# Queries turned two heads at a time, their squares summed by halving additions on POOL

## The chip, the cores and the metric

One core of a Trainium2 chip runs the whole kernel. The metric is the device time of one execution in microseconds (us). The engines are PE (TensorE, the matrix unit), ACT (ScalarE), DVE (VectorE), POOL (GpSimd) and SP (SyncE, which here only starts DMAs). Each engine works through its own queue in order, and they wait for each other by semaphores.

## What is computed

One layer of a bidirectional encoder over two sequences of 512 tokens with width 1024: an attention branch (16 heads of 64, four key and value heads, a window of 128 tokens to both sides) and a state-space branch run from the same normed input, are gated and added, and a squared-ReLU MLP follows. What matters here is the attention's queries:

```python
h = rms_norm(x, ln1)
proj = h @ w_in
q, k, v, u, g_att, g_ssm = jnp.split(proj, IN_SPLITS, axis=-1)
q = rms_norm(q.reshape(bsz, seq_len, N_HEADS, HEAD_DIM), q_gain)   # over each head's 64 numbers
k = rms_norm(k.reshape(bsz, seq_len, N_KV_HEADS, HEAD_DIM), k_gain)
...
s = einsum(q, k) * scale + bias      # then masked, with a sink logit, softmax, times v
```

## The kernel before

Matrix products are made in float32 precision from two parts: a number is split into a high part (rounded to the matrix unit's float32 format) and a low part (the rest), and three products (high by high, high by low, low by high) are added in PSUM. Where both parts of one operand fit on the partitions together, one product does two: a head has 64 numbers, so a query's high part lies on partitions 0 to 63 and its low part on 64 to 127, and the keys are held twice, once on either half (`kh` the high part in both halves, `kl` the low). A score matmul with `kh` and one with `kl` then give the sum of all four products, whichever half of the query lies on which rows.

The attention works in eight steps (four groups of four heads, two sequences each), and a step in four units of 128 query rows. A unit (class `Unit`) makes for each of its four heads the scores (`scores`, L970), the bias and the row's maximum (`largest`, DVE, L974), the exponentials (`exp`, ACT, L980), and, one unit later, turns the probabilities (`turn`, PE, L986), splits them into parts (`high`, ACT, L990; `low`, DVE, L995), multiplies by the values (`value`, PE, L1002) and adds the two halves (`lower_part`, ACT, L1006; `add`, DVE, L1012).

Beside it runs one query tile for the next step (class `Tile`): 128 rows by four heads of 64. Its way goes through all engines:

- `project`: 24 matmuls of 256 columns, spread over the unit (PE, L919)
- `square`: squares of the projection, scaled (ACT, L925), at the end of the unit
- `power`: sum of each head's 64 squares (DVE, L929), plus epsilon (POOL, L931), to the power of -0.5 (POOL, L932); at the start of the next unit
- `norm`: projection times that factor (DVE, L936), in that unit, behind two maxima, an addition and a low part on DVE
- `turn`: four transposes, one for each head (PE, L941), behind the fourth head's scores
- `high` and `low`: the copy with the gain (ACT, L946) and the rest (DVE, L949)

The order of the instructions on PE, ACT, DVE and POOL is the order in which the loop writes them out. At a unit's start stand `power`, low parts for a later stage (`y_lows`, POOL, L1066, from step 6 on), then `scores(0)`, `largest(0)` and so on. The core of a unit's loop is:

```python
project(6)
if n3:
    prev.low(0)
cur.exp(0)
cur.exp(1)
if rows and not rows.qn:
    rows.norm()
...
if rows:
    rows.turn()
```

POOL also copies the sink logits into each unit's row block (L962), copies keys once a step (L888), subtracts high parts of weights (L874, L786) and issues some DMAs (L1170). DVE has, from the second step on, two more operations of 1024 columns on SBUF in each step: the gate's multiplication at the end of the third unit (`gated`, L1047) and the one by the reciprocal sums at the end of the fourth (`multiply`, L1051). Ahead of the eight steps stands a front in which the four tiles of the first step are made between the projections of the values (`rows_block`, `v_evac`). In the eighth step there are no tiles.

Of the kernel before, what the change touches and what calls it, by code (L numbers as in the profile page):

```python
# [12 lines left out]
F32 = mybir.dt.float32  # L13
F32R = mybir.dt.float32r
I32 = mybir.dt.int32
AF = mybir.ActivationFunctionType
ALU = mybir.AluOpType
AX = mybir.AxisListType

P = 128  # L20
# [10 lines left out]
G = 4  # L31
HD = 64
# [32 lines left out]
def hybrid_layer(ctx, tc, x, x_t, w_kv, rel, onehot, w_qkv, w_ug, vectors, lam, coefs, w_glu, w_out, ln2,  # L65
                 w_up, w_down, out):
    nc = tc.nc
    V, S, PE, GP, SP = nc.vector, nc.scalar, nc.tensor, nc.gpsimd, nc.sync
# [12 lines left out]
    def acc():  # L81
        return ps_acc.tile([P, 512], F32, tag="acc", name="acc")
# [23 lines left out]
    ident = const.tile([P, P], F32, name="ident")  # L106
# [5 lines left out]
    bglu_sb, gain_q, gain_k, nsink = [vec[:, a:b] for a, b in ((0, 8), (8, 9), (9, 10), (10, 26))]  # L112
# [422 lines left out]
    with tc.tile_pool(name="hst", bufs=1) as hp:  # L535
        h = hp.tile([P, NCHUNK, 2, GROUPS, NSEQ], F32, name="h")
# [148 lines left out]
        with tc.tile_pool(name="ssmo", bufs=2) as sp:  # L685
# [54 lines left out]
            for q in range(GROUPS // SH):  # L740
# [7 lines left out]
                for g in range(SH):  # L748
                    o = ps[:, g * P:(g + 1) * P]
# [88 lines left out]
    with tc.tile_pool(name="att", bufs=2, reuse_waits="tile") as ap, tc.tile_pool(name="attc", bufs=1, reuse_waits="tile") as ac:  # L838
# [18 lines left out]
        weights, keys, queries, biases = {}, {}, {}, {}  # L857
# [48 lines left out]
        class Tile:  # L906
# [19 lines left out]

            def power(self):
                ms = small.tile([P, G], F32, tag="ms", name="ms")
                V.reduce_sum(ms, self.sq, axis=AX.X)  # L929
                self.rq = small.tile([P, G], F32, tag="rq", name="rq")  # L930
                GP.tensor_scalar_add(ms, ms, EPS)  # L931
                GP.tensor_tensor(self.rq, ms, neg_half[:, 0:G], op=ALU.pow)  # L932
# [4 lines left out]

            def turn(self):
                self.pt = self.pt or acc()
                for h in range(G):  # L940
                    PE.transpose(self.pt[0:64, h * P:(h + 1) * P], self.qn[:, h], ident)  # L941

            def high(self):
                self.ptv = self.pt[0:64].rearrange("p (h t) -> p h t", h=G)
                self.dst = queries[self.key][:, :, self.t * P:(self.t + 1) * P]
                S.activation(self.dst[0:64], self.ptv, AF.Copy, scale=gain_q[0:64])  # L946

            def low(self):
                V.scalar_tensor_tensor(self.dst[64:128], self.ptv, gain_q[0:64], self.dst[0:64].bitcast(F32),  # L949
                                       op0=ALU.mult, op1=ALU.subtract)  # L950

        class Unit:

# [149 lines left out]
        with tc.manual_schedule(engines={ET.PE, ET.DVE, ET.Activation, ET.Pool}):  # L1103
# [11 lines left out]
            ms, rk = [small.tile([P, NB * N_KV], F32, tag="rsum", name=n, bufs=2) for n in ("k_ms", "k_rs")]  # L1115
# [45 lines left out]
        with tc.manual_schedule(engines={ET.PE, ET.Activation, ET.DVE, ET.Pool}):  # L1161
            for i, (j, sq) in enumerate(steps):
# [4 lines left out]
                for qb in range(NB):  # L1167
                    if 1 <= i < 3:
                        t = (i - 1) * NB + qb
# [213 lines left out]
    with tc.tile_pool(name="rn2", bufs=2, reuse_waits="tile") as rn2:  # L1383
# [51 lines left out]
        def put_turned(sq, t, last=lambda: None, between=()):  # L1435
# [9 lines left out]
            def put(dst, src):  # L1445
                high(dst, src)
                next(inner, lambda: None)()
                low(dst, src)
# [10 lines left out]
            if not between:  # L1459
                S.copy(tt[0], x11)  # L1460
                high(B22, x22)
                V.tensor_sub(tt[0], x12, tt[0])
                low(B22, x22)
                high(T1, tt[0])
                V.tensor_sub(tt[1], x22, tt[0])
                low(T1, tt[0])
                high(T2, tt[1])
                S.copy(tt[0], x22)
                low(T2, tt[1])
                V.tensor_sub(tt[0], tt[0], x12)  # L1470
                high(T3, tt[0])
                V.tensor_sub(tt[1], tt[1], x21)
                high(T4, tt[1])
                last()
                low(T3, tt[0])
                low(T4, tt[1])
                xb.clear()
                return
# [47 lines left out]
        def parts(src, owed=None):  # L1526
            i = next(turn) % KT
            hi, lo = [q[:, i, :].rearrange("p (k n) -> p k n", k=4) for q in ring]
            S.copy(hi, src)
            low = lambda: V.tensor_sub(lo, src, hi.bitcast(F32))  # L1530
            low() if owed is None else owed.append(low)
            return hi, lo
# [325 lines left out]
```

## Time and profile before

| | us |
|---|---|
| median of 3 runs | 1445.42 (1445.25 to 1445.69) |
| the profiled execution | 1445.04 |
| its span, first instruction to last | 1443.3 |
| busy PE, DVE, ACT, POOL | 1435.6, 1094.9, 762.3, 244.1 |
| granted clock of the matrix unit | 1.00 throughout |

The attention with its front lies between 408 and 661 us of the span; ahead of it are the projections and the state-space scan, behind it the gated sum and the MLP. A row of the timeline gives the start and the length in us, the engine, the line, the operation, what it writes and reads, the shape and the number of instructions that the row merges; in brackets stand the idle time before it and what ended it. A row of the groups gives the count, the busy us, the mean ns of one, the idle time before and what ended it. The shape on a PE row is that of the weights (128\*64) and of the moving operand.

### The profile page before, as it was taken

To read this page: it belongs to the slowest core of one execution; us is meant where nothing else is said; L and a number is where in the kernel's file an instruction comes from. 1 tells how busy PE (TensorE), PEld (TensorE's weight loads), DVE (VectorE), ACT (ScalarE), POOL (GpSimd) and SP (SyncE) were. 2 spreads that over 40 slices of the span, in tenths; PEclk is the share of its full clock that TensorE was granted. 3 is DMA by queue.
4 is the path that set the end of the run, shared out by engine and by line. 5 is a ranking of instruction groups with operands and counts; after the bars stand their busy time and mean duration, and the time that the engine had idled before them with its cause. 6 is when DMAs were issued, how large, how long until landed. Compare 5 with 4: busy or idle time off the path is not lost.

```text
span 1443.3 us, 22044 instructions
## 1 busy us (share of the span) xinstructions
PE 1435.6 (99%) x7997; PEld 1228.0 (85%) x7997; DVE 1094.9 (76%) x1978; ACT 762.3 (53%) x1359; POOL 244.1 (17%) x396
## 2 busy tenths in 40 slices
PE   9999999999999999999999999999999999999998
PEld 8888888889999999988888888888888888888887
DVE  7999959995458999988976588777776597575644
ACT  7678861224448887894444255455454443333332
POOL 3144443004244432263100000000000000000000
PEclk9999999999999999999999999999999999999999
DMA  7356549529651533345552344444442983464341
GB/s 297 97 170 189 168 147 327 206 91 314 227 180 59 162 107 100 119 140 189 194 190 91 129 136 173 161 160 155 151 143 96 363 319 102 146 201 145 121 131 59
DMA packets 102204, 240.23 MB, mean 166 GB/s; under 512 B 12330, under 2 KB 25130, under 8 KB 102096
## 3 DMA queue, kind: packets, MB, share of 16 engines
q1 hardware_dynamic: 62304, 139.94, 29.9%
q0 software_dynamic: 16320, 48.28, 10.2%
q10 hardware_dynamic: 23472, 50.61, 9.5%
q8 instruction: 63, 1.03, 0.3%
q14 instruction: 45, 0.37, 0.1%
HBM read 169.02 MB, written 81.82 MB: 174 GB/s over the span
## 4 chain that ended last, share of the span: by engine, by line
PE 84%; DVE 8%; issue 4%; DMA 2%; ACT 1%; POOL 1%; DVEq 0%; SPq 0%; ACTq 0%; POOLq 0%
PE bank L118 14%; PE bank L120 14%; PE bank L119 14%; PE acc L187 9%; PE acc L125 6%; PE acc L919 5%; PE po L1002 2%; PE sps L970 2%; PE sps L641 2%; PE tps L986 2%; PE sps L753 2%; PE acc L120 2%; PE acc L119 2%; PE acc L118 2%; DVE t L716 2%
## 5 line engine op out<-in xcount | busy, mean ns | idle before, releaser
L187 PE MATMUL acc<-act,c_hi 128*128 128x512 f32 x768 | 243.7, 395 | 0.0
L119 PE MATMUL bank<-b_lo,a_hi 128*128 128x512 f32 (+1 forms) x449 | 174.4, 389 | 0.0
L120 PE MATMUL bank<-b_hi,a_lo 128*128 128x512 f32 (+1 forms) x449 | 174.4, 389 | 0.0
L118 PE MATMUL bank<-b_hi,a_hi 128*128 128x512 f32 (+1 forms) x449 | 174.4, 389 | 0.0
L187 PEld LDWEIGHTS acc<-act,c_hi 128*128 128x128 f32 x768 | 142.3, 188 | 27.8 <-ACT act L316 0.9
L1714 ACT CAST a_hi<-d_a 128x1024 fp32r<-128x1024 f32 x56 | 59.1, 1055 | 177.4 <-PE bank L119 173.2
L187 PE MATMUL acc<-act,c_lo 128*128 128x512 f32 x384 | 151.3, 394 | 0.0
L1715 DVE TENSOR_TENSOR a_lo<-d_a,a_hi 128x1024 fp32r<-128x1024 f32 x56 | 68.5, 1223 | 98.5 <-ACT a_hi L1714 98.5
L118 PE MATMUL bank<-act,act 128*128 128x512 f32 x368 | 143.2, 389 | 0.0
L119 PE MATMUL bank<-act,act 128*128 128x512 f32 x368 | 143.2, 389 | 0.0
L120 PE MATMUL bank<-act,act 128*128 128x512 f32 x368 | 143.2, 389 | 0.0
L919 PE MATMUL acc<-w_hi,act 128*128 128x256 f32 x512 | 114.0, 291 | 0.1
L119 PEld LDWEIGHTS bank<-b_lo,a_hi 128*128 128x128 f32 x449 | 84.3, 188 | 17.5
L120 PEld LDWEIGHTS bank<-b_hi,a_lo 128*128 128x128 f32 x449 | 84.3, 188 | 17.5
L118 PEld LDWEIGHTS bank<-b_hi,a_hi 128*128 128x128 f32 x449 | 84.3, 188 | 17.3
L919 PEld LDWEIGHTS acc<-w_hi,act 128*128 128x128 f32 x512 | 87.0, 189 | 4.0 <-PE sps L970 0.3
L187 PEld LDWEIGHTS acc<-act,c_lo 128*128 128x128 f32 x384 | 72.2, 188 | 14.7 <-DVE c_lo L178 0.8
L125 PE MATMUL acc<-act,gc_hi 128*128 128x512 f32 x256 | 81.2, 394 | 0.3 <-POOL act L1066 0.3
L118 PEld LDWEIGHTS bank<-act,act 128*128 128x128 f32 x368 | 69.1, 188 | 14.4
L120 PEld LDWEIGHTS bank<-act,act 128*128 128x128 f32 x368 | 69.1, 188 | 14.3
L119 PEld LDWEIGHTS bank<-act,act 128*128 128x128 f32 x368 | 69.1, 188 | 14.2
L980 ACT ACTIVATE p<-p,nmx 128x257 f32<-128x257 f32 (+1 forms) x128 | 72.0, 563 | 16.5 <-DVE nmx L974 15.5
(365 smaller groups left out, 3424.4 us busy)
## 6 DMA issues: line engine op xcount, KB each, us to landing
d_a<-a_scr SPq DMA_DIRECT2D x56, 512.0 KB, 3.6
raws<-in_w_up_dram SPq DMA_DIRECT2D x32, 512.0 KB, 4.0
a_scr<-t ACTq DMA_DIRECT2D x64, 256.0 KB, 3.0
k<-in_w_down_dram SPq DMA_DIRECT2D x32, 512.0 KB, 5.6
c_raw<-in_w_ug_dram SPq DMA_DIRECT2D x48, 256.0 KB, 4.1
ct_scr<-ctab POOLq DMA_DIRECT2D x16, 512.0 KB, 4.8
ctab_in<-ct_scr POOLq DMA_DIRECT2D x16, 512.0 KB, 6.4
a_scr<-a ACTq DMA_DIRECT2D x32, 256.0 KB, 2.0
```

Of the source, the lines that this page charges most:

```text
L118: PE.matmul(ps, a[0], b[0], start=first, stop=False)
L119: PE.matmul(ps, a[0], b[1], start=False, stop=False)
L120: PE.matmul(ps, a[1], b[0], start=False, stop=last)
L125: PE.matmul(ps, w[wi][:, k, :], rows[yi], start=k + p == 0, stop=k == KT - 1 and p == 2)
L187: PE.matmul(ps, w[wi][:, k, :], hT[s][hi][:, k, :], start=n == 0, stop=n == 3 * KT - 1)
L641: PE.matmul(ps[:, i * P:(i + 1) * P], bm[:, ri, g, :], u_sb[:, gp * SH + g, :], start=True, stop=True)
L716: V.tensor_mul(t1, h[:, i], a8r)
L753: PE.matmul(o, ctab[:, g0 % SI + g, ri, 0:T * CH], st[:, ri, g].rearrange("p s k -> p (s k)"), start=False, stop=ri == 1)
L919: PE.matmul(self.ps, hT[sq][act][:, k, col:col + P], w[:, k % 4, :], start=i == 0, stop=i == 3 * KT - 1)
L980: S.activation(p, p, AF.Exp, bias=self.nmx[:, h:h + 1], scale=-1.0, accum_out=self.sums[:, h, self.qb:self.qb + 1])
L1714: S.copy(hi, src)
L1715: V.tensor_sub(lo, src, hi.bitcast(F32))
```

## The change

- `power`: the sum of a head's 64 squares is made on POOL by halving: 32 columns added to 32, then 16, 8, 4, 2 (in place), and a last addition of two columns into `ms`. In all heads at once, so 128, 64, 32, 16, 8 and 4 numbers on each partition. DVE's reduction goes away.
- `turn`: two transposes of 128 columns, each with two heads side by side, in place of four of 64. An even head comes out on partitions 0 to 63 and an odd one on 64 to 127.
- `high` and `low`: each becomes two operations of two heads. For even heads the high part lies on the lower rows and the low part on the upper, as before; for odd heads the high part stays on the upper rows and the low part goes to the lower.

```diff
             def power(self):
                 ms = small.tile([P, G], F32, tag="ms", name="ms")
-                V.reduce_sum(ms, self.sq, axis=AX.X)
+                n = HD // 2
+                while n > 1:
+                    GP.tensor_tensor(self.sq[:, :, 0:n], self.sq[:, :, 0:n], self.sq[:, :, n:2 * n], op=ALU.add)
+                    n //= 2
+                GP.tensor_tensor(ms, self.sq[:, :, 0], self.sq[:, :, 1], op=ALU.add)
                 self.rq = small.tile([P, G], F32, tag="rq", name="rq")
                 GP.tensor_scalar_add(ms, ms, EPS)
                 GP.tensor_tensor(self.rq, ms, neg_half[:, 0:G], op=ALU.pow)
...
             def turn(self):
                 self.pt = self.pt or acc()
-                for h in range(G):
-                    PE.transpose(self.pt[0:64, h * P:(h + 1) * P], self.qn[:, h], ident)
+                for e in range(2):
+                    PE.transpose(self.pt[:, e * P:(e + 1) * P],
+                                 self.qn[:, 2 * e:2 * e + 2].rearrange("p o d -> p (o d)"), ident)
 
             def high(self):
-                self.ptv = self.pt[0:64].rearrange("p (h t) -> p h t", h=G)
-                self.dst = queries[self.key][:, :, self.t * P:(self.t + 1) * P]
-                S.activation(self.dst[0:64], self.ptv, AF.Copy, scale=gain_q[0:64])
+                ptv = self.pt[:, 0:2 * P].rearrange("p (e t) -> p e t", e=2)
+                dst = queries[self.key][:, :, self.t * P:(self.t + 1) * P].rearrange("p (e o) t -> p e o t", o=2)
+                self.parts = []
+                for o in range(2):
+                    own, other = [slice(i * 64, (i + 1) * 64) for i in (o, 1 - o)]
+                    self.parts.append((dst[other, :, o], ptv[own], gain_q[own], dst[own, :, o]))
+                    S.activation(dst[own, :, o], ptv[own], AF.Copy, scale=gain_q[own])
 
             def low(self):
-                V.scalar_tensor_tensor(self.dst[64:128], self.ptv, gain_q[0:64], self.dst[0:64].bitcast(F32),
-                                       op0=ALU.mult, op1=ALU.subtract)
+                for lo, src, gain, hi in self.parts:
+                    V.scalar_tensor_tensor(lo, src, gain, hi.bitcast(F32), op0=ALU.mult, op1=ALU.subtract)
```

## The prediction

> **What bounds the kernel now.** I read the page's first part, then the busy times by stage, the groups of the attention stage, the chain that ended last, and then the timeline of single units there.
>
> ```profile
> span 1443.3 us, 22044 instructions
> PE 1435.6 (99%) x7997; PEld 1228.0 (85%) x7997; DVE 1094.9 (76%) x1978; ACT 762.3 (53%) x1359; POOL 244.1 (17%) x396
> 463.00:493.00 30.00, 29.95 (x226) 28.00 (x224) 27.34 (x71) 24.09 (x63) 14.65 (x23) 1.00 0.56 177
> 467.28 0.71 PE sps L970 x4
> 495.39 0.70 PE sps L970 x4
> ```
>
> The third line is a stretch of 30 us in the stage that the change touches (busy PE, weight loads, DVE, ACT, POOL). PE is never idle, and DVE is close behind with 27.3. POOL has half its time free. The rows of the chain mark the start of the same unit in two successive steps of four units: 28.1 us a step, about 7 a unit, seven steps with a query tile each unit, and a front of four tiles before them. So whatever PE saves in a unit is time, if nothing that PE waits for gets later. What it waits for is a chain through all engines, here of one plain unit (two answers of the timeline for PE and one each for the others):
>
> ```profile
> 445.80 0.28 PE L919 MATMUL acc<-w_hi,act 128*128 128x256 f32 x1
> 446.18 0.39 ACT L925 ACTIVATE sq<-acc 128x256 f32<-128x256 f32 x1 [0.68 <-PE acc L919]
> 446.60 0.42 DVE L929 TENSOR_REDUCE ms<-sq 128x4 f32<-128x256 f32 x1 [0.91 <-ACT sq L925]
> 447.11 0.23 POOL L931 TENSOR_SCALAR ms<-ms 128x4 f32<-128x4 f32 x1 [3.23 <-DVE ms L929]
> 447.42 1.04 POOL L932 TENSOR_TENSOR rq<-ms,neg_half 128x4 f32<-128x4 f32 x1
> 449.49 0.41 DVE L936 TENSOR_TENSOR qn<-acc,rq 128x256 f32<-128x256 f32 x1
> 450.10 0.60 PE L941 MATMUL acc<-ident,qn 128*64 128x128 f32 x4
> 450.53 0.60 PE L986 MATMUL tps<-ident,p 128*128 128x128 f32 x4
> 452.75 0.28 PE L919 MATMUL acc<-w_hi,act 128*128 128x256 f32 x1
> ```
>
> Call P the last projection matmul of a tile (445.80). Its transposes start at 450.10, which is P + 4.30. PE has other matmuls all that while. The factor rq is ready at 448.46, DVE takes it up at 449.49 because its queue comes to it only then, and the normed tile is done at 449.90. The chain therefore has 1.03 us of slack before DVE's norm and 0.20 behind it. After the transposes the next P comes at 452.75, 2.65 later.
>
> In two of four units of steps 1 to 6 the gate's multiplication (L1047) or the one by the reciprocal sums (L1051) stands on DVE just behind the square, and there the turn waits for the norm already:
>
> ```profile
> 480.58 0.28 PE L919 MATMUL acc<-w_hi,act 128*128 128x256 f32 x1
> 480.90 0.39 ACT L925 ACTIVATE sq<-acc 128x256 f32<-128x256 f32 x1 [0.22 <-PE acc L919]
> 481.02 1.22 DVE L1047 TENSOR_TENSOR ya<-ya,gate 128x1024 f32<-128x1024 f32 x1
> 484.76 0.41 DVE L936 TENSOR_TENSOR qn<-acc,rq 128x256 f32<-128x256 f32 x1
> 485.24 0.51 PE L941 MATMUL acc<-ident,qn 128*64 128x128 f32 x3
> 487.91 0.29 PE L919 MATMUL acc<-w_hi,act 128*128 128x256 f32 x1
> 488.21 1.22 DVE L1051 TENSOR_TENSOR ya<-ya,fac 128x1024 f32<-128x1024 f32 x1
> 492.43 0.62 PE L941 MATMUL acc<-ident,qn 128*64 128x128 f32 x4
> ```
>
> P to turn is 4.66 and 4.52 there. The step is 2 x 4.30 + 4.66 + 4.52 plus four ways from turn to next P.
>
> **The change part by part.** Turn: four transposes become two. Four take 450.10 to 450.53, 0.43, so two fewer save 0.215 a tile, 32 x 0.215 = 6.9 us if PE stays the bound. Their weight loads grow from 64 to 128 columns:
>
> ```profile
> L941 PEld LDWEIGHTS acc<-ident,qn 128*64 128x64 f32 x116 | 11.9, 111 | 3.3
> L986 PEld LDWEIGHTS tps<-ident,p 128*128 128x128 f32 x288 | 33.2, 140 | 0.7
> L946 ACT ACTIVATE qa<-acc,vec 64x512 fp32r<-64x512 f32 x29 | 19.5, 673 | 0.2 <-PE acc L941 0.2
> L949 DVE SCALAR_TENSOR_TENSOR qa<-acc,vec,qa 64x512 fp32r<-64x512 f32 x30 | 22.3, 745 | 5.9 <-ACT qa L946 5.6
> L1012 DVE TENSOR_TENSOR ya<-po,ol 64x256 f32<-64x256 f32 x56 | 23.2, 415 | 0.4
> ```
>
> That is 0.03 more for each load, beside a running matmul, so the saving lies between 0.16 and 0.22; I take 0.215, since eight full transposes of L986 run at the same pace.
>
> High and low: one ACT copy of 0.673 becomes two of 64x256. The square above moves 256 columns in 0.39, so 0.77, 0.1 more; ACT has 6 of 30 us idle. One DVE operation of 0.745 becomes two, each between 0.415 (L1012, same shape) and 0.745 x 0.65, so 0.83 to 0.97, up to 0.2 more. The first low can start when half of the high is done, which pays the ACT part back. All of it lies behind the turn, with the next unit's scores as reader, several us on.
>
> Sums: DVE loses L929, 0.42 a tile, so with the lows about 0.2 less in all. POOL gets six additions, over 128, 64, 32, 16, 8 and 4 numbers a partition, each reading the one before. Prices:
>
> ```profile
> 38.11 0.61 POOL L513 TENSOR_TENSOR vec<-vec,ident 128x16 f32<-128x16 f32 x2
> L1066 POOL TENSOR_TENSOR act<-act,act 128x512 fp32r<-128x512 f32 x16 | 20.4, 1292 | 4.5 <-ACT act L1069 4.4
> 646.07 0.61 POOL L1065 CAST act<-act 128x512 fp32r<-128x512 f32 x1
> 646.76 1.30 POOL L1066 TENSOR_TENSOR act<-act,act 128x512 fp32r<-128x512 f32 x1
> 610.05 2.53 POOL L1066 TENSOR_TENSOR act<-act,act 128x512 fp32r<-128x512 f32 x2
> 612.55 1.29 POOL L786 TENSOR_TENSOR gc_lo<-c_raw,gc_hi 128x512 fp32r<-128x512 f32 x1
> ```
>
> Two dependent additions of 16 numbers take 0.61, one of 512 takes 1.29. A dependent POOL operation starts 0.08 after the end of the one before (646.68 to 646.76; 447.34 to 447.42). So one of 16 is (0.61 - 0.08) / 2 = 0.26, or 0.22 if the first of the pair was slow, and the slope is (1.29 - 0.22) / 496 = 2.16 ns a number. That makes 0.46, 0.33, 0.26, 0.22, 0.21 and 0.20, together 1.67, and 2.15 with six gaps. Lower end 1.43, if they follow each other like independent ones (the operation at 612.55 starts 0.03 before the pair ahead of it, 610.05 + 2.53, has ended); upper end 2.75, if four short rows cost more than one long one, which no row shows. I take 2.15, the value nearest to the dependent pair.
>
> Plain unit: square done 446.57, additions from 446.60 to 448.75, then 0.31 + 1.04 as now, rq at 450.10, norm 450.13 to 450.54, turn 450.60. P to turn is 4.80 in place of 4.30. DVE would have been ready near 449.1 (0.42 less in its queue), so it now stands 1 us at the norm, and behind it stand the second two maxima, the low parts and with them PE's value matmuls; they have that much room in a unit of 7 us. Net 0.50 - 0.215 = +0.285.
>
> Gate units: L1047 and L1051 read two SBUF tiles, and so do the additions. The trace shows what that does:
>
> ```profile
> 665.30 3.41 POOL L786 TENSOR_TENSOR gc_lo<-c_raw,gc_hi 128x512 fp32r<-128x512 f32 x2 [2.57 <-ACT gc_hi L785]
> 666.04 1.52 DVE L813 TENSOR_TENSOR gs<-gs,yy 128x512 f32<-128x512 f32 x1
> 667.59 1.67 DVE L830 TENSOR_TENSOR ga<-ga,gs 128x512 f32<-128x512 f32 x1
> 674.41 0.69 DVE L813 TENSOR_TENSOR gs<-gs,yy 128x512 f32<-128x512 f32 x1
> ```
>
> Two POOL subtractions take 3.41 in place of 2.6 and the DVE products beside them 1.52 and 1.67 in place of 0.69: they take turns. [...] With the lows after it DVE reaches L1047 near P + 0.8 and L1051 near P + 0.65, and the square is done at P + 0.7, so at most one addition gets in and the rest waits until about P + 1.95: 1.95 + 2.15 + 1.35 + 0.03 + 0.41 + 0.06 = 5.9, and 5.8. Net 5.9 - 4.66 - 0.215 = +1.03 and 5.8 - 4.52 - 0.215 = +1.07.
>
> Front: here DVE's norm stands right at the factor, and the last of its four tiles is on the path to the first unit.
>
> ```profile
> 431.07 0.38 ACT L925 ACTIVATE sq<-acc 128x256 f32<-128x256 f32 x1
> 432.68 1.04 POOL L932 TENSOR_TENSOR rq<-ms,neg_half 128x4 f32<-128x4 f32 x1
> 435.53 0.38 PE L970 MATMUL sps<-kh,qa 128*128 128x256 f32 x1 [0.26 <-DVE nmx L974]
> ```
>
> Rq goes from 433.72 to 431.48 + 2.15 + 1.35 = 434.98, 1.26 later, and with it PE's third pair of scores, plus 0.2 for the lows, less three turns of 0.215: +0.8.
>
> Sum: front 0.8; step 0 (no gate) 4 x 0.285 = 1.1; steps 1 to 6, 6 x (0.57 + 1.03 + 1.07) = 16.0; together +17.9. The profiled execution took 1445.04 (span 1443.3 and 1.7 around it), 0.4 below the median 1445.42. I predict 1463. Step 6 may add up to 2, since POOL has more behind the factor there (the rows from 610.05 on, 3.8 us): factor at P + 4.3, then 3.8 and a copy is P + 8.3, beyond a unit of 7.3 to 8.
>
> **The rivals.** N, no turn-taking with the gates: the chain takes 4.74 in all gate units (the square starts 0.06 sooner there); 0.57 - 0.13 + 0.0 a step, 6 x 0.44 + 1.1 + 0.8 = +4.6, 1450. For it: before, no POOL operation lies beside L1047 or L1051 in this stage, so the case itself isn't shown. Against it: the four rows above.
>
> B, additions back to back, 1.43: plain units are hidden (4.08 against 4.30, so -0.215 each), gate units 5.2 and 5.1, +0.33 and +0.37; 6 x 0.27 - 0.9 - 0.1 = +0.6, 1446, no change. [...]
>
> H, the other side: the chain stays hidden, at every unit, and PE keeps its 0.215. [...] Then up to 6.9 us less, 1438.5; the 1.03 us of slack speaks for it.
>
> U, short rows dear, 2.75: 28 x 0.6 = +17 on top, 1479.
>
> **How the numbers follow.** About 0.2%, 3 us, is what can be told from no change. Forecast (1453 to 1470) 0.62, N 0.10, B 0.06, H 0.08, U 0.14. Slower: 0.62 + 0.10 + 0.14 = 0.86; same 0.06; faster 0.08. The range leaves B, H and the far end of U out: 1449 to 1477.
>
> **What would show it.** In the changed profile: two transposes 0.11 apart; six POOL additions between square and the 0.23 operation, 2.15 from first start to it; DVE idle before the norm, put down to POOL's rq, about 1 us in plain units; P to turn 4.8, and near 5.8 in gate units, the first or second addition stretched there by 0.5 to 1.2; a step of 30.8 in place of 28.1. If additions start at 0.25 each and DVE's norm never waits, the prediction is wrong, and H holds. The part after the attention should keep its lengths.

## The result, and the profile after

| | before | after |
|---|---|---|
| median of the runs | 1445.34 (1445.16 to 1445.69, 4 runs) | 1477.81 (1476.54 to 1478.15, 4 runs) |
| span of the profiled execution | 1443.3 | 1476.2 |
| busy POOL | 244.1 | 309.1 |

The ratio is 1.0224 (95% interval 1.0208 to 1.024): 32.5 us slower. The direction was forecast, the size was not: 1463 was predicted, with 1477 as the upper end of the range. Each experiment below is held against the kernel before as measured beside it (medians of 1444.52 to 1445.02), and one slow execution, of e11 with 4644.47 us, is left out of its ratio. The page of the changed kernel, its first lines and the chain that ended last by engine:

```profile
span 1476.2 us, 22197 instructions
PE 1438.4 (97%) x7933; PEld 1221.2 (83%) x7933; DVE 1096.7 (74%) x1978; ACT 771.9 (52%) x1391; POOL 309.1 (21%) x588
...
PE 73%; DVE 10%; POOL 6%; issue 6%; ACT 4%; DMA 1%; DVEq 0%; SPq 0%; POOLq 0%; ACTq 0%
```

PE's busy time hardly moved; its idle time is what came. In the attention stage it shows in 30 us that lie like those of the prediction (busy PE, weight loads, DVE, ACT, POOL):

```profile
493.00:523.00 30.00, 26.81 (x195) 24.22 (x193) 24.14 (x65) 22.57 (x59) 19.63 (x43) 1.00 0.49 149
```

PE was never idle there before; now it is busy for 26.8 of 30 us, and DVE too has fallen, from 27.3 to 24.1. Both wait. The list of waits between 433 and 660 us says for what (us in total, times, longest):

```profile
ACT p L989 <- DVE nmx L983: 36.8, 41, 1.9
DVE qn L940 <- POOL rq L936: 24.3, 26, 3.1
PEld acc L945 <- DVE qn L940: 23.2, 24, 1.5
```

The order is the chain's: POOL's factor, DVE's norm, PE's turn, and behind DVE's wait the maxima that ACT's exponentials need. One plain tile (no gate's product beside it), from the timelines of PE, ACT, POOL and DVE:

```profile
475.51 0.28 PE L919 MATMUL acc<-w_hi,act 128*128 128x256 f32 x1
476.13 0.38 ACT L925 ACTIVATE sq<-acc 128x256 f32<-128x256 f32 x1
476.59 1.79 POOL L931 TENSOR_TENSOR sq<-sq 128x128 f32<-128x128 f32 x5 [1.41 <-ACT sq L925]
478.46 0.20 POOL L933 TENSOR_TENSOR ms<-sq 128x4 f32<-128x4 f32 x1
478.75 0.23 POOL L935 TENSOR_SCALAR ms<-ms 128x4 f32<-128x4 f32 x1
479.06 1.04 POOL L936 TENSOR_TENSOR rq<-ms,neg_half 128x4 f32<-128x4 f32 x1
480.14 0.42 DVE L940 TENSOR_TENSOR qn<-acc,rq 128x256 f32<-128x256 f32 x1 [0.88 <-POOL rq L936]
480.62 0.44 PE L945 MATMUL acc<-ident,qn 128*128 128x128 f32 x2 [0.67 <-DVE qn L940]
482.78 0.28 PE L919 MATMUL acc<-w_hi,act 128*128 128x256 f32 x1
```

The six additions take 476.59 to 478.75, 2.16, which is the predicted 2.15, and DVE stands 0.88 before the norm. But P to turn is 5.11, not 4.80, and the part of it that wasn't foreseen is at the top: the square ends at P + 1.00, where it ended at P + 0.77 before, and its row names no wait, so it followed on ACT's own work. A gate tile:

```profile
490.65 0.28 PE L919 MATMUL acc<-w_hi,act 128*128 128x256 f32 x1
491.89 1.22 DVE L1056 TENSOR_TENSOR ya<-ya,gate 128x1024 f32<-128x1024 f32 x1
491.93 2.81 POOL L931 TENSOR_TENSOR sq<-sq 128x128 f32<-128x128 f32 x5 [2.00 <-ACT sq L925]
496.50 0.42 DVE L940 TENSOR_TENSOR qn<-acc,rq 128x256 f32<-128x256 f32 x1 [1.11 <-POOL rq L936]
496.98 0.44 PE L945 MATMUL acc<-ident,qn 128*128 128x128 f32 x2 [0.72 <-DVE qn L940]
```

The same five additions that took 1.79 take 2.81 beside the gate's product, which started 0.04 before them and itself stays at 1.22. P to turn is 6.33. The groups of this tile by shape put the whole of it in the first addition, which took 0.46 in the plain tile:

```profile
L931 POOL TENSOR_TENSOR sq<-sq 128x128 f32<-128x128 f32 x1 | 1.5, 1487 | 2.0 <-ACT sq L925 2.0
```

In the tile after it the first addition starts before the product by the reciprocal sums. There the second addition is the long one (1.19 for 0.32), and the product is held up too, 1.47 for 1.22:

```profile
500.39 2.63 POOL L931 TENSOR_TENSOR sq<-sq 128x128 f32<-128x128 f32 x5 [2.93 <-ACT sq L925]
500.45 1.47 DVE L1060 TENSOR_TENSOR ya<-ya,fac 128x1024 f32<-128x1024 f32 x1
```

The groups of 433 to 660 us, for the turn's parts:

```profile
L959 DVE SCALAR_TENSOR_TENSOR qa<-acc,vec,qa 64x256 fp32r<-64x256 f32 x56 | 27.1, 483 | 11.5 <-ACT qa L955 10.5
L955 ACT ACTIVATE qa<-acc,vec 64x256 fp32r<-64x256 f32 x58 | 26.9, 464 | 0.4
L945 PE MATMUL acc<-ident,qn 128*128 128x128 f32 x58 | 12.4, 296 | 15.2 <-DVE qn L940 15.2
```

A high copy of half the size takes 0.464 where the whole took 0.673, a low 0.483 where the whole took 0.745.

Where the time came from, by stretches between the last projection matmuls (P) of tiles 0, 4, 8 and 28, each as its difference from before, in us of the profiled execution (before: front 27.44, step 0 27.98, steps 1 to 5 140.42; the last column is the rest of the span, 1247.5). The rows below after are experiments:

| | front | step 0 | steps 1-5 | rest |
|---|---|---|---|---|
| predicted | 0.8 | 1.1 | 13.4 | 2.7 |
| after | 6.1 | 2.8 | 20.6 | 3.4 |
| e1, sums on POOL alone | 4.6 | 1.9 | 15.1 | 1.7 |
| e2, turns alone | 0.0 | 1.1 | 7.5 | 1.6 |
| e3, front's sums by DVE | 0.0 | 3.4 | 20.3 | 3.8 |
| e4, no two-operand gate product | 4.6 | 2.7 | 11.9 | 0.9 |
| e13, turns with one high copy | 0.0 | 0.5 | 2.4 | 1.6 |
| e15, the change with one high copy | 7.7 | 1.4 | 14.0 | 2.3 |

### The profile page after: what moved, and what is told of

Read it like the earlier page. It is cut to its first block, busy times and chain, and to the rows that moved or that the text cites. A ratio compares the mean times of both kernels' runs of the same rounds, so it can differ in the third digit from the quotient of the medians.

```text
span 1476.2 us, 22197 instructions
## 1 busy us (share of the span) xinstructions
PE 1438.4 (97%) x7933; PEld 1221.2 (83%) x7933; DVE 1096.7 (74%) x1978; ACT 771.9 (52%) x1391; POOL 309.1 (21%) x588
## 4 chain that ended last, share of the span: by engine, by line
PE 73%; DVE 10%; POOL 6%; issue 6%; ACT 4%; DMA 1%; DVEq 0%; SPq 0%; POOLq 0%; ACTq 0%
PE bank L118 14%; PE bank L120 14%; PE bank L119 14%; PE acc L187 10%; PE acc L125 6%; POOL sq L931 2%; POOL rq L936 2%; PE sps L641 2%; PE acc L919 2%; PE sps L753 2%; DVE t L716 2%; PE acc L120 1%; PE acc L118 1%; PE acc L119 1%; DVE t L718 1%
## 5 line engine op out<-in xcount | busy, mean ns | idle before, releaser
L919 PE MATMUL acc<-w_hi,act 128*128 128x256 f32 x512 | 115.6, 294 | 4.9 <-DVE qn L940 4.9
L919 PEld LDWEIGHTS acc<-w_hi,act 128*128 128x128 f32 x512 | 88.2, 192 | 9.0 <-DVE qn L940 3.7
L187 PEld LDWEIGHTS acc<-act,c_lo 128*128 128x128 f32 x384 | 72.2, 188 | 15.1 <-DVE c_lo L178 1.1
```

The lines of the kernel that those rows point to most:

```text
L187: PE.matmul(ps, w[wi][:, k, :], hT[s][hi][:, k, :], start=n == 0, stop=n == 3 * KT - 1)
L919: PE.matmul(self.ps, hT[sq][act][:, k, col:col + P], w[:, k % 4, :], start=i == 0, stop=i == 3 * KT - 1)
```

## The experiments

### The two parts alone: e1 and e2

e1 is the change without its turns, e2 the change without its sums:

```
e1: turn(), high(), low() as before
e2: V.reduce_sum(ms, self.sq, axis=AX.X)     # for the six GP additions
```

> The sums on POOL alone; turn, high and low as in the kernel before. Theory L (loop: the late factor holds DVE's norm, behind it the third maximum, its exponential, the copies of the high part and so the next tile's square on ACT): the loop doesn't pass PE, so the two transposes more cost little, and the one high copy is 0.3 us shorter on ACT than the two, so the square is earlier: 1472 to 1478, the square's end near P + 0.8 to 1.0 in place of 1.0 to 1.3. Theory S (the parts add up on PE, as in the prediction): after plus 32 x 0.17 to 0.215, 1483 to 1485.

Measured: 1468.67, ratio 1.0165 (1.015 to 1.018), 24.1 slower. The prediction's term for the additions without the two transposes was 17.9 + 6.9 = 24.8. The time lies below both expectations. Both took the change's turns to save time or to be hidden, which e2 doesn't bear out.

> The turn, high and low of the change alone; the sum by DVE's reduction as before. Both theories: DVE's norm never waits for the factor. Theory L: the plain units gain 0.17 us each (from turn to next P 2.49 in place of 2.65), the gate units lose that again to the 0.24 us more of the low parts on DVE, about 1442 to 1444. Theory S: 28 x 0.17 and the front, 1440. A third, that the split copies are what costs (theory C): the square late by 0.3 us on ACT already, and above 1448.

Measured: 1456.67, ratio 1.0082 (1.0067 to 1.0097), 12.2 slower. The part that was to save 6.9 costs 12, as the third theory's "above 1448" had it. Alone the two parts lose 36.3, together 32.5. The turn to next P is 2.16 and 2.48 in e2, 2.32 and 2.65 before: two transposes fewer do save 0.16 to 0.17 a tile. What took it back is seen in one tile of e2 (PE, ACT and DVE):

```profile
531.38 0.44 PE L941 MATMUL acc<-ident,qn 128*128 128x128 f32 x2
532.73 0.94 ACT L951 ACTIVATE qa<-acc,vec 64x256 fp32r<-64x256 f32 x2
533.54 0.28 PE L919 MATMUL acc<-w_hi,act 128*128 128x256 f32 x1
533.70 0.98 DVE L955 SCALAR_TENSOR_TENSOR qa<-acc,vec,qa 64x256 fp32r<-64x256 f32 x2 [0.64 <-ACT qa L951]
534.43 0.38 ACT L925 ACTIVATE sq<-acc 128x256 f32<-128x256 f32 x1
534.85 0.42 DVE L929 TENSOR_REDUCE ms<-sq 128x4 f32<-128x256 f32 x1 [0.16 <-ACT sq L925]
538.34 0.43 PE L941 MATMUL acc<-ident,qn 128*128 128x128 f32 x2
```

The two high copies take 0.94 together, the lows start when both are done (533.67), and the next square, two ACT operations on, ends 1.27 behind P (534.43 + 0.38 - 533.54). P to turn is 4.80 where it was 4.29. Two engines are late at the same point, ACT for the square and DVE for the lows; e13 tells them apart.

### The front and the gates: e3, e4, e8

e3 is the change with the four tiles of the front summed by DVE; in e4 and e8 (on the change and on before) a reduction of 1024 numbers of one SBUF tile stands in the place of the gate's and the sums' products, in all steps but the last, so both leave these products out:

```
e3: if self.key == (0, 0): V.reduce_sum(ms, self.sq, axis=AX.X)
...
e4, e8: - V.tensor_mul(self.ya, self.ya, self.ga)          # where not self.last; multiply() likewise
        + V.reduce_sum(small.tile([P, 1], ...), self.ga.rearrange("p m t -> p (m t)"), axis=AX.X)
```

> The change, but the first step's four tiles (the front) summed by DVE's reduction. If the front costs what the trace of after shows (6.1 us from the first P to the fifth, since PE's next projection takes the PSUM bank that the late norm still reads, and the matmuls behind the wait ran at a granted clock of 0.66): 1471 to 1473, and no granted clock below 1 in the front. If the front costs the 0.8 us of the prediction and the rest of the 6 us is passed on anyway: 1476 to 1477.

Measured: 1472.42, ratio 1.0191 (1.0174 to 1.0208): 5.4 off the change's time (4.6, each against its own kernel before), and the front is at 27.43 again. The prediction gave the front 0.8. In the changed kernel DVE's norm waits 3.1 to 3.7 for the factor there, where it waited 1.5 before, and behind two of these waits PE waits too (timelines of DVE and PE):

```profile
421.36 0.42 DVE L940 TENSOR_TENSOR qn<-acc,rq 128x256 f32<-128x256 f32 x1 [3.70 <-POOL rq L936]
421.84 0.39 PE L919 MATMUL acc<-w_hi,act 128*128 128x256 f32 x1 [1.51 <-DVE qn L940]
429.34 0.42 DVE L940 TENSOR_TENSOR qn<-acc,rq 128x256 f32<-128x256 f32 x1 [3.39 <-POOL rq L936]
429.82 0.39 PE L919 MATMUL acc<-w_hi,act 128*128 128x256 f32 x1 [1.74 <-DVE qn L940]
```

The instruction that waits is a projection (L919), not the turn: the next tile's accumulator is the one that the norm still has to read. The prediction followed the last of the four tiles to the scores, and passed over the accumulators of the first three.

> The change, with the two multiplications of 1024 columns by the gate and by the reciprocal sums left out of steps 1 to 6, and in their place a reduction over 1024 numbers each, as long on DVE (1.22 us) but with one SBUF tensor read in place of two. If POOL and DVE take turns because of two SBUF inputs: all six additions take 2.15 us in the gate units too (3.18 and 3.01 in after), 12 tiles less by 0.85 to 1.03 us, 1466 to 1468. If the stretch comes from something else that lies there (DVE's load, the square's place): 1477, additions as in after.

Measured: 1466.37, ratio 1.0152 (1.0136 to 1.0167), 11.4 off the change's time (10.6, each against its own kernel before). The same gate tile in e4 (DVE and POOL):

```profile
489.68 1.21 DVE L1059 TENSOR_REDUCE ss<-gate 128x1 f32<-128x1024 f32 x1
489.71 1.77 POOL L931 TENSOR_TENSOR sq<-sq 128x128 f32<-128x128 f32 x5 [2.01 <-ACT sq L925]
```

DVE works as long, 1.21 for 1.22, and starts at the same point, but with one SBUF operand it leaves POOL's additions alone: 1.77 against 2.81. The reduction also writes one number a row, not 1024. That writing alone doesn't hold POOL up is seen in the plain tile of the changed kernel, where DVE's maximum reads PSUM and the bias, writes 384 columns to SBUF, and the first addition beside it (476.59) still takes 0.46:

```profile
476.52 0.62 DVE L983 CUSTOM_DVE_ANT_0 p<-sps,bias,vec 128x384 f32<-128x384 f32 x1
```

> Control for e4: the kernel before with the gate products (two operands of 1024 numbers a row, lines 1047 and 1051) replaced by a reduction of one operand of 1024, for every unit pair but the last, so that the products are left out. Theory V (e4's -11.4 us come from VectorE and GpSimd taking turns in SBUF, which before has none of, since GpSimd adds little there): 1441 to 1449, as before. Theory W (the reduction is simply cheaper in its place): 1432 to 1437, as far below before as e4 is below the change.

Measured: 1445.29 against 1444.92, ratio 1.0002 (0.9993 to 1.0011). The reduction isn't cheaper than the product where POOL has no additions, so what e4 takes off is the taking of turns: 10.6 to 11.4, about a third of the change's loss.

### Why the turns cost: e6, e11, e9, e10

e6 and e11 keep the four transposes of before and split the copies by heads, e6 both, e11 the low alone; e9 and e10 move a cast from ACT to POOL, in e2 and in before:

```
e6:  for m in (slice(0, 2), slice(2, 4)):
         S.activation(self.dst[0:64, m], self.ptv[:, m], AF.Copy, scale=gain_q[0:64])
     ... (the low part in the same way; e11: the low part only)
e9, e10: - S.copy(hi[:, sl, :], raw)
         + GP.tensor_copy(hi[:, sl, :], raw)
```

> The kernel before with its four transposes a tile, only that the high copy and the low part are each two operations of two heads (64 x 256) where they were one of four (64 x 512). Theory C (two smaller operations on each engine, and their taking of turns over one PSUM tile, are the cost of the turns part): slower by that cost without what two fewer transposes save; with e2's +12.2 us and a saving of 0.17 us a tile over 32 tiles that is 1457 to 1463. Theory T (the cost comes with the transposes over 128 columns, that write all 128 rows): within 3 us of before, 1443 to 1449.

> As e6, but only the low part is in two operations; the high copy is one again. If VectorE's 0.24 us more ahead of the gate products is what e6 lost (12 gate tiles x 0.24 us = 2.9, and something at the ends): 1447.5 to 1450, as e6. If ScalarE's 0.15 us more did it: 1444.5 to 1446.

Measured: e6 1449.2, ratio 1.0031 (1.0019 to 1.0044), 4.3 slower; e11 1447.23, ratio 1.0015 (1.0006 to 1.0025), 2.2 slower. e6 lies at the upper end of theory T, far under C, and e11 just under the first of its own ranges: the split by itself is a third of e2's loss, and about half of that is the low part's, whose pair takes 0.87 there (0.98 in e2). With four transposes ACT's two copies take 0.82 together, and plain tiles don't notice:

```profile
530.61 0.82 ACT L947 ACTIVATE qa<-acc,vec 64x256 fp32r<-64x256 f32 x2
...
532.11 0.38 ACT L925 ACTIVATE sq<-acc 128x256 f32<-128x256 f32 x1
```

Here the square still ends at P + 0.77 (P is 531.73), without its 0.2 of waiting: the 0.15 more was just covered. In e2 it is 0.27 more, and P comes 0.17 sooner for two transposes fewer; 0.27 + 0.17 - 0.21 is 0.23 by this estimate, and the squares of e2 end 0.22 late in the first tile of a step and, with that handed on, 0.51 late in the second.

> As e2 (turns by two heads, VectorE's own sum), but the weights' cast to w_hi (128x512, 0.62 us on ScalarE, in the first two tiles of each step; line 873) is done by GpSimd, which is idle there. Theory A (ScalarE's line of work is full in those two tiles: the 0.27 us more of a turn's two copies, and the 0.17 us by which TensorE is earlier, exceed its 0.21 us of idle time, and the lateness is handed on from tile to tile): square at P+0.7 to P+0.8 again, P to turn 4.3 in plain tiles, steps of about 28.0 instead of 29.6, and 1441 to 1447. Theory B (VectorE's 0.24 us more for the lows in every tile is enough): plain tiles stay at 4.5/4.8 and the time at 1453 to 1458.

> Control for e9: the kernel before with the same cast on GpSimd. By theory A ScalarE has 0.2 us to spare at each square there, so nothing is gained: 1443 to 1446. If it gains like e9 does, the cast has a cost of its own.

Measured: e9 1455.25, ratio 1.0072 (1.006 to 1.0085), not to be told from e2; e10 1445.62, ratio 1.0006 (0.9997 to 1.0014). Theory A fell, and e9 lies in the range of B. 0.62 us less on ACT between one square and the next changes no tile, since the exponentials behind the cast wait for DVE's maxima (0.65 in e9's trace, where e2 has 0.22): ACT isn't short of time over the unit, only between the turn and the square.

### The high copies as one: e13 and e15

A copy of all 128 rows into both columns of a pair costs ACT one operation; the halves that don't belong are overwritten by the lows:

```
- S.activation(dst[own, :, o], ptv[own], AF.Copy, scale=gain_q[own])     # for o in 0, 1
+ S.activation(every, ptv[:, :, None, :].to_broadcast([P, 2, 2, P]), AF.Copy, scale=gain_q)
```

> As e2 (turns by two heads, VectorE's own sum), but the high copies are one operation again: 128 rows x 512 numbers, every row's pair of columns written to both heads of the pair, where the two low parts then overwrite the halves that belong to them; nothing is left out. ScalarE's work per tile is that of before (0.67 us for a turn, not 0.94), VectorE's stays that of e2 (0.98 us for the lows). Theory H (e2's loss is the split of the high copies, which the square and the lows both follow): square ends at P+0.8, plain tiles at P to turn 4.3 with 0.17 us a tile saved, gate tiles still 0.1 to 0.3 late for the lows: 1442 to 1448. Theory L (the lows' 0.24 us on a VectorE that has no idle time from P to the turn): 1452 to 1457.

Measured: 1449.3, ratio 1.0029 (1.0017 to 1.004), 4.5 slower: 7.6 of e2's 12.2 are gone, and the time lies 1.3 above the range of theory H. The same tile as above (PE, ACT, DVE):

```profile
529.73 0.43 PE L941 MATMUL acc<-ident,qn 128*128 128x128 f32 x2
531.08 0.68 ACT L949 ACTIVATE qa<-acc,vec 128x512 fp32r<-128x512 f32 x1
531.79 0.98 DVE L956 SCALAR_TENSOR_TENSOR qa<-acc,vec,qa 64x256 fp32r<-64x256 f32 x2 [0.37 <-ACT qa L949]
531.90 0.28 PE L919 MATMUL acc<-w_hi,act 128*128 128x256 f32 x1
532.28 0.39 ACT L925 ACTIVATE sq<-acc 128x256 f32<-128x256 f32 x1
532.81 0.42 DVE L929 TENSOR_REDUCE ms<-sq 128x4 f32<-128x256 f32 x1
536.29 0.44 PE L941 MATMUL acc<-ident,qn 128*128 128x128 f32 x2
```

The square ends at P + 0.77 again. DVE's sum starts at P + 0.91, now directly behind the lows (531.79 + 0.98), where it started at P + 0.80 before and P + 1.31 in e2, and P to turn is 4.39. Plain tiles now gain a little (6.60 and 6.90 from P to P, 6.62 and 6.95 before); the gate tiles, whose products stand behind the lows, lose 0.22 to 0.36. So the larger part of e2's loss was the two copies on ACT. For the rest the trace points to DVE: its lows take 0.24 more and P comes 0.17 sooner, and the gate's product starts at P + 0.96 where it started at P + 0.43. No run with two transposes takes the lows' 0.24 away, so this part is read, not shown.

> The change as it is (sums on GpSimd too), with the high copies as one operation as in e13. Theory H: it takes off the change about what it takes off e2, 8 to 12 us: 1466 to 1470. Theory L, or if the wait for GpSimd's sums covers the later square: 1474 to 1478.

Measured: 1468.93, ratio 1.0162 (1.0146 to 1.0178), 8.9 off the change's time (8.3, each against its own kernel before), in the range of theory H and no less than it took off e2: POOL's sums don't cover a late square, they start with it. With the squares at P + 0.8 again, P to turn is 4.88 in plain tiles and 5.71 and 5.80 in gate tiles, where the prediction had 4.80, 5.9 and 5.8, and steps 1 to 5 lose 14.0 where it had 13.4.

### Other places for the same work: e5, e7, e12, e14, e16

```
e5:  rows.high() behind new.square(); rows.low() behind the next unit's norm()
e7:  norm() behind largest(2); turn() and high() behind value(1, 0); low() at the unit's end
e12: e9, with rows.low() behind gated() and multiply() in the gate tiles
e14: e13, with cur.exp(2) behind rows.high();  e16: before, with the same order
```

> As e2 (turns by two heads, VectorE's own sum), but a turn's two high copies are issued behind the next tile's square on ScalarE, and its two low parts behind the next unit's norm on VectorE. Theory A (e2's +12.2 us come from the order: ScalarE gives the copies first, so the next square ends at P+1.0 to P+1.3 where it ended at P+0.77, and the sum and norm are late by that): the square ends at P+0.8 again, P to turn falls from 4.5/4.8 to about 4.2 in plain tiles, and the time is 1440 to 1446. Theory B (it is VectorE's and ScalarE's added work, 0.25 us a tile on each, wherever it stands): 1452 to 1458, the gate products as late as in e2.

> As e2, but a tile's norm stands behind the unit's third maximum, its turn and high copies behind the value product of the unit's first heads, and its low parts at the unit's end. Theory A (what matters is that norm, turn and copies don't stand between a unit's maxima and its exponentials): TensorE no longer waits for the norm and two fewer transposes show, 1437 to 1446. Theory B (the engines' work rules): 1452 to 1458. A new wait, the next unit's scores for the low parts, would make it 1460 or more.

> As e9, and in the two tiles of a step with gate products the low parts stand behind these on VectorE. If both causes are named rightly, every tile saves what two transposes cost (0.17 us) and nothing is given back: 1438 to 1443, under the kernel before. If the scores of the next unit then wait for the lows, or the lows delay that unit's maxima, it's 1445 or more.

> As e13, and the high copy stands ahead of the unit's third exponential on ScalarE, so that the lows can follow 0.7 us earlier on VectorE and are done before the gate products. Theory H: gate tiles too save their 0.17 us: 1438 to 1444. Rival: the later exponentials hold up the square or the transposes of the probabilities: 1446 or more.

> Control for e14: the kernel before with its high copy ahead of the third exponential. Its squares wait for TensorE (0.2 us) and its lows have time: 1443 to 1446. If it is faster than that, e14's gain isn't the turns'.

Measured, as ratio to before: e5 1467.05, 1.0155 (1.0141 to 1.0169); e7 1464.78, 1.0138 (1.0124 to 1.0152); e12 1463.6, 1.013 (1.0116 to 1.0144); e14 1451.82, 1.0049 (1.0036 to 1.0061); e16 1450.33, 1.0037 (1.0025 to 1.005). Every one is slower than the order it came from, none came into the range in which it was to help, and the control e16 lies above its range. In e5 the square does end at P + 0.8, as was asked of it, and the time still rises by 10: the lows, now ahead of the maxima, make ACT's exponentials wait 43.3 us for DVE between 433 and 660, against 18.5 in e2. In e12 the gate products start 0.4 sooner and the sum 0.7 later. In e16 the kernel before loses 5.6 by that order alone, so e14, 2.5 above e13, says nothing against e13's reading. In the tile of e2 above DVE is idle for 0.2 us between the start of its lows and the turn, so it seems that whatever is put in there sooner makes something else late. None of these versions, and none of the others, beats the kernel before.

## Why the prediction missed

**Bound and mechanism: right.** PE waits for the norm 24 times and the norm for POOL 26 times between 433 and 660 us, so in nearly every tile, and the additions' 2.15 us are in the trace of a plain tile to 0.01. The turn-taking with the gate's products is there, with 10.6 to 11.4 us by e4; the forecast stood 17.9 - 4.6 = 13.3 above rival N, which left it out. That an addition waits until a product is through was the prediction's estimate from its four rows; in the changed kernel the first addition took 1.49 for 0.46 beside a product of 1.22. In e4, with one SBUF operand and the same DVE time (1.21 for 1.22), the stretch is gone, 1.77 for 2.81; in e8, without POOL's additions, the same exchange took nothing off (ratio 1.0002). With one high copy (e15) the way from P to the turn is within 0.2 us of the forecast in every unit of steps 1 to 5. Rival B's time isn't borne out: the additions don't follow back to back. The groups of 433 to 660 us by shape, with the idle time before each in the last column:

```profile
L931 POOL TENSOR_TENSOR sq<-sq 128x16 f32<-128x16 f32 x28 | 6.2, 223 | 2.2
L933 POOL TENSOR_TENSOR ms<-sq 128x4 f32<-128x4 f32 x28 | 5.7, 203 | 2.2
```

Each addition behind the first has 2.2 us of gaps in 28 tiles, 0.08 each time, and the short rows cost what the forecast took (0.22 and 0.20). What makes the 0.08, no row shows.

**The additions' term: right by luck, by errors that cancel.** 24.8 was worked out, 24.1 measured (e1). But its front is 4.6 where the prediction, without the transposes, had 0.8 + 4 x 0.215 = 1.7; its steps 1 to 5 are 15.1 where the prediction's terms, likewise, give 5 x (2 x 0.50 + 1.24 + 1.28) = 17.6; and its rest is 1.7 where step 6 alone was to give 3.5.

**The step that failed: high and low.** The prediction priced the halves from other operations' rows (0.39 for the square, so 0.77 and 0.1 more for the pair; 0.83 to 0.97 for the lows), had the first low start at half of the high, and put all of it "behind the turn, with the next unit's scores as reader, several us on". Measured: 0.94 for the pair of copies, 0.27 more; 0.98 for the lows, just above the upper price; the lows start when both copies are done. And the scores are not the first reader that matters. The next tile's square stands behind these copies on ACT, the sum and the gate products behind the lows on DVE, and the square had 0.21 us to spare (the 0.22 in the row of the prediction's gate unit shows it). The term stood at 0 and the transposes at -6.9; together they measured +12.2 (e2), of which e13 gives 7.6 to the copies.

**The transposes: the lower end.** 0.16 to 0.17 a tile, of 0.16 to 0.22: from the turn to the next matmul it is 0.27 (480.62 to 480.89), where four transposes took 0.43.

**The front: mis-sized.** 6.1 for 0.8. The last of its tiles, the one that the prediction followed, costs 1.3 (10.61 from P to P for 9.30). What was left out is that two projections wait for an accumulator, 1.51 and 1.74. The other 1.5 goes with the clock, at 0.66 from 430 to 435 us (below); in e1 and e4, where it was 1.00 there, the front is 4.6.

**Step and signs.** The step is 32.24 (475.51 to 507.75), not 30.8. One of the prediction's sums comes out otherwise from its own figures: 1.67 less six times the 0.03 that it names is 1.49, not rival B's 1.43. It doesn't bear on the result. DVE's idle time at the norm is 0.88 and 1.11, near the 1 us named. The prediction's list of what would show it held on POOL, with the first or second addition stretched by 1.0 and 0.9 in gate tiles. It had no sign for ACT, because it looked at no row behind the turn.

What stays open: how much of e13's 4.5 the lows alone make, why two parts that lose 36.3 apart lose 32.5 together, and what of the last tiles and the passage out of the attention makes the 1 to 2 us more in the rest of the span, were not taken apart.

## What to carry to other kernels

When an operation is split in two, price the pair by its own kind and read, on each of its engines, which instruction stands behind it and how long that one waited before: that idle time, not the distance to the reader of its result, is the cover. A saving on the bounding engine makes the next deadline earlier and uses up the same cover: here P came 0.17 sooner and the square had 0.21. And a buffer that is read late holds up whoever writes it next, here two projection matmuls of the front by 1.51 and 1.74, away from the chain that the prediction followed.

## What the runs showed of the hardware

A copy from PSUM with a scale on ACT takes 0.464 for 64 rows x 256 numbers (after), 0.673 for 64 x 512 (before) and 0.675 for 128 x 512 (e13): twice the rows cost no more here, and half the numbers cost 0.69 of the time. Two of the half copies in a row take 0.82 when both read the same 64 rows (e6), and 0.94 when the second reads the other 64 and each writes every other head (e2); twice 0.464 is 0.93.

The granted clock fell in the front of the changed kernel and not in e4's, behind the same idle times of PE (window, busy PE, weight loads, DVE, ACT, POOL, clock; first the change, then e4 with its own two rows of PE):

```profile
430.00:435.00 5.00, 5.00 (x31) 5.00 (x32) 2.32 (x4) 0.08 (x1) 0.00 (x0) 0.66 0.02 3
```

```profile
421.23 0.38 PE L919 MATMUL acc<-w_hi,act 128*128 128x256 f32 x1 [1.51 <-DVE qn L940]
429.18 0.39 PE L919 MATMUL acc<-w_hi,act 128*128 128x256 f32 x1 [1.74 <-DVE qn L940]
```

```profile
430.00:435.00 5.00, 5.00 (x45) 5.00 (x44) 2.45 (x4) 1.78 (x4) 1.00 (x3) 1.00 0.02 3
```

In these 5 us PE ran 31 matmuls at 0.66 and 45 at 1.00; a tile's projection took 4.35 from its first to its last matmul there (429.82 to 434.17) and 2.86 a tile earlier (421.84 to 424.70). In e15 the clock was at 0.66 in this stretch and in one more of the front (440 to 445), which goes with its 7.7 in the table. So behind the same idle times of 1.5 and 1.7 us, 8 us apart, the clock fell in one execution and stayed in another; that they are what lowers it isn't shown. In the changed kernel it went down with no single idle time of PE above 1.74 us in the front before it, and no run shows what decides.
